# Where the weight buffers and the activation buffers of a two-layer decoder trunk begin in SBUF

## The chip, the cores and the metric

The kernel runs on one core of a Trainium2 chip. The metric is device time in microseconds (us) from the start to the end of one execution. Three executions of the kernel before took 626.92, 623.93 and 623.89 us; the median is 623.93 us.

## The reference

The reference is a decoder trunk of two layers on 256 tokens of 1024 features, all in float32. Every sub-layer is x + gate * f(rmsnorm(x) * (1 + scale) + shift), where shift, scale and gate are columns of silu(c) @ w_ada + b_ada.

```
for i in range(2):
    sh_m, sc_m, g_m, sh_f, sc_f, g_f = split(silu(c) @ w_ada[i] + b_ada[i], 6)
    h = rmsnorm(x) * (1 + sc_m) + sh_m
    y = attention(h)          # layer 0: 8 heads, causal, QK norm
        or short_conv(h)      # layer 1: (B * conv3(C * u)) @ w_out
    x = x + g_m * y
    h = rmsnorm(x) * (1 + sc_f) + sh_f
    x = x + g_f * ((silu(h @ w_gate) * (h @ w_up)) @ w_down)   # d_ff = 2816
```

## The kernel before

**The products.** Each float32 operand of a large product is held as two float32r parts: a high part and the rest. A product then takes three matmuls (`mm3`, lines 287 to 289): high by high, high weight by low moving, low weight by high moving. Each loads its own 128 x 128 stationary operand and streams 256 columns of 1024 bytes per partition past it. There are 4704 such matmuls. 

**The weights.** They come from HBM in chunks of 256 columns, in the order of their use. A chunk lands in a `wf` buffer (five of them); ScalarE writes its high part into a `wh` tile and VectorE the rest into a `wl` tile (`prep`, `split_w`, lines 88 to 99). There are three `wh` and three `wl` buffers, taken in turn, and each part of a chunk is 8192 bytes per partition. A chunk is asked for two chunks ahead of its use (`produce`, `get`).

**The activations.** They lie feature-major in pairs of tiles, a high and a low part. `new_pair("h", ...)` holds the modulated input of a sub-layer: q, k, v, gate, up and the convolution's input products read it (names `m0`, `f0`, `m1`, `f1`). `new_pair("a", ...)` holds the 22 x 256 values between up and down projection, which the down projection reads (`a0`, `a1`, output `op_d`). `wide_pair` holds tag `z`: the attention's output and the convolution's output, read by the two output projections (`ov`, `zv`, outputs `op_o`, `op_co`). The first gate and up chunks of a sub-layer work on a raw pair, which lies at the end of an `a` pair or in a `z` pair and has 258 columns, so that its eight blocks begin 1032 bytes apart (outputs `raw_f`, `raw_m`).

**Where the tiles lie.** The tiles of a pool are laid one behind the other, in the order in which their tags are first asked for, each starting at a multiple of 32 bytes. Behind the five `wf` buffers come the three `wh`, the three `wl`, and then the activations `al`, `zh`, `xT`, `hh`, `hl`, `zl`, `ah`. All of them are a multiple of 128 bytes long but `zh` and `zl`, which have 8256 bytes (64.5 times 128).

**What sets the order.** TensorE works through its instructions in the program's order; where each chunk's split and load stand on ScalarE, VectorE and SyncE's DMA queue follows from `get` and `produce`. A `wh` or `wl` buffer is written again once the products of the chunk three turns earlier have read it.

Of the kernel before, what the change touches and what calls it, by code (L numbers as in the profile page):

```python
# [15 lines left out]
P = 128  # L16
S = 256
# [14 lines left out]
def trunk_kernel(ctx: ExitStack, tc: tile.TileContext, x, c, w_ada, b_ada, norm_mix, norm_ffn, w_qkv, w_o,  # L32
# [20 lines left out]

# [1 line left out]
    crow = const.tile([KD, P], F32, name="crow")  # L55
# [24 lines left out]

# [1 line left out]
    def load(src, nk, ncol, name):  # L82
# [3 lines left out]
        return flat  # L86

    def prep(src, nk, name):
        wf = load(src, nk, CW, "wf_" + name)
        wh = wpool.tile([P, 8, CW], F32R, tag="wh", name="wh_" + name, bufs=3)  # L90
        wl = wpool.tile([P, 8, CW], F32R, tag="wl", name="wl_" + name, bufs=3)
        split_w(wf, wh, wl, nk)
        return wh, wl
# [6 lines left out]

# [1 line left out]
    mod = const.tile([P, DEPTH * 48], F32, name="mod")  # L102
# [3 lines left out]
    def ada_piece(l, part, i):  # L106
        w = load(w_ada[l, i * 256:(i + 1) * 256, part * D:(part + 1) * D], 2, D, f"wa_{l}_{part}_{i}")
        if i == 0:
            acc_of[l, part] = tmp.tile([P, D], F32, tag="acc", name=f"acc_{l}_{part}", bufs=1)
        acc = acc_of[l, part]  # L110
        for kk in range(2):
            k = 2 * i + kk
            if k == 0:
                nc.vector.tensor_scalar(acc, w[:, kk], sc[:, k:k + 1], None, op0=ALU.mult)
            else:
                nc.vector.scalar_tensor_tensor(acc, w[:, kk], sc[:, k:k + 1], acc, op0=ALU.mult, op1=ALU.add)  # L116
        if i < 3:
            return
        if l == 0 and part != G_F:
            late.append((gets[0], lambda: ada_end(l, part, acc)))  # L120
            return
        # the sum over the partitions, of three bfloat16 parts that add up to the float32 values: less for PE
        parts = [tmp.tile([P, D], BF16, tag=f"part{n}", name=f"part{n}_{l}_{part}", bufs=1) for n in range(3)]
        for n, p in enumerate(parts):
            if n < 2:
                nc.scalar.activation(p, acc, AF.Copy)
                nc.vector.tensor_sub(acc if n == 0 else parts[2], acc, p)
        late.append((gets[0], lambda: ada_end_parts(l, part, parts)))

    def ada_end(l, part, acc):  # L130
        # the sum over the partitions, on four groups of 32 columns of the array at once: less for DVE and ScalarE
        ps = ps_misc(f"mod_ps_{l}_{part}")[:, :2 * P]
        for g in range(4):
            nc.tensor.matmul(ps[32 * g:32 * g + 32], one.to_broadcast([P, 32]), acc[:, g * 2 * P:(g + 1) * 2 * P],
                             start=True, stop=True, skip_group_check=True, tile_position=(0, 32 * g))
        y = tmp.tile([P, 2, P], F32, tag="t", name=f"mod_y_{l}_{part}", bufs=3)
        nc.scalar.activation(y, ps.rearrange("p (i c) -> p i c", c=P), AF.Copy)

        def end():
            ps = ps_misc(f"mod_c_{l}_{part}")  # L140
            for i in range(2):
                nc.tensor.transpose(ps[:, i * P:(i + 1) * P], y[:, i], ident)
            mod_from(ps[:, :2 * P].rearrange("p (i g r) -> p g i r", i=2, r=32)[:, :, :, 0], l, part)

        return end
# [41 lines left out]

    rows = act.tile([P, 3 * P], F32, tag="al", name="rows")
    brow, vrow, grow = (rows[:n, i * P:(i + 1) * P] for i, n in enumerate((DEPTH * 48, 42, 16)))
    x_flat = act.tile([P, KD * (S + 2)], F32, tag="zh", name="x_tok")  # L190
    x_tok = x_flat[:, :2 * D].rearrange("p (t d) -> p t d", d=D)
# [16 lines left out]

# [1 line left out]
    chunks = []  # L210
# [72 lines left out]

# [1 line left out]
    def mm3(ps, lhs, rhs, first, last):  # L285
# [25 lines left out]
    def new_pair(tag, name, nk):  # L311
        return (act.tile([P, nk, S], F32R, tag=tag + "h", name=name + "h"),
                act.tile([P, nk, S], F32R, tag=tag + "l", name=name + "l"))

    # A raw pair holds x * (1 + scale) * gain, not yet over its norm, and the shift as one more token (twice, for an
    # even number of them). Products of it need no norm; rstd and the product of the shift come to them afterwards:
    # (x A rstd + sh) W = (x A) W rstd + sh W.
    RAW = KD * (S + 2)

    def wide_pair(name):  # L320
        flat = [act.tile([P, RAW], F32R, tag="z" + p, name=name + p) for p in "hl"]
        return (tuple(f[:, :KD * S].rearrange("p (k s) -> p k s", s=S) for f in flat),
                tuple(f.rearrange("p (k s) -> p k s", s=S + 2) for f in flat))
# [4 lines left out]

# [1 line left out]
    xT = act.tile([P, KD, S], F32, name="xT")  # L330
# [20 lines left out]
    class Norm:  # L351
        """Sums of squares over the features, gathered as the residual's tiles come."""

# [83 lines left out]
    def raw_gemm(keys, norm, name):  # L437
        """Two chunks' products of the raw pair; returns (product * rstd, the shift's product) of each, and
        the modulated pair. The norm's own products come in between."""
        raw = norm.raw  # L440
# [43 lines left out]

# [1 line left out]
    def mod_sums(w, name):  # L486
        # Four groups of 32 columns of the array hold four rows of c at once: partial sums in four groups of partitions.
        n = w.shape[1]
        ps = ps_misc("mod_ps_" + name)
        psv = ps[:, :n * P].rearrange("p (n c) -> p n c", c=P)  # L490
        for k in range(KD):
            g = 32 * (k % 4)
            nc.tensor.matmul(psv[g:g + 32], sc[:, k:k + 1].to_broadcast([P, 32]), w[:, :, k], start=k < 4, stop=k >= 4,
                             skip_group_check=True, tile_position=(0, g))
        y = tmp.tile([P, 2, P], F32, tag="t", name="mod_y_" + name, bufs=3)[:, :n]
        nc.vector.tensor_copy(y, psv)
        return y

    def group_sums(ps, y, name):
        # the four groups' partial sums added up, as columns  # L500
        n = y.shape[1]
# [37 lines left out]
    def w_operands(k, wf):  # L539
        ops = (wpool.tile([P, 8, CW], F32R, tag="wh", name=f"wh_qk_{k}", bufs=3),  # L540
               wpool.tile([P, 8, CW], F32R, tag="wl", name=f"wl_qk_{k}", bufs=3))
        w_part(wf, ops, 0, 2)
        return ops
# [6 lines left out]
    def first_products(k, ops, js):  # L550
        wh, wl = ops
        for j in js:
            for t in range(2):
                ts = slice(t * P, (t + 1) * P)
                # q feature-major, k token-major
                if j < 4:
# [9 lines left out]
    def keep_warm(n):  # L566
        # The array's clock falls while it idles: products that nothing reads keep it up until the first operands are there.
        ps = ps_misc("warm")
# [4 lines left out]
    with tc.manual_schedule(engines={mybir.EngineType.PE, mybir.EngineType.DVE, mybir.EngineType.Activation}):  # L573
# [4 lines left out]
        nc.vector.tensor_copy(mask_r, causal)  # L578
        # brings the table of square roots in before the first one is needed
        std = const.tile([P, 2], F32, name="std0")  # L580
        nc.scalar.activation(std[:, 0:1], eps, AF.Sqrt)
        keep_warm(14)
        w_ada0, wf = first
        sq = act.tile([P, RAW], F32, tag="zl", name="sq0")
        ssq = const.tile([P, 2], F32, name="ssq0")
# [50 lines left out]

# [1 line left out]
    qT = act.tile([P, 2, H, S], F32, tag="ah", name="qkT")  # L638
    vp = act.tile([P, 2 * D + H * 3 * P], F32, tag="al", name="vp")
    v_sb = vp[:, :2 * D].rearrange("p (t d) -> p t d", d=D)  # L640
# [23 lines left out]
    def q_sums(ps, a):  # L664
        # Four heads at once, on 32 columns of the array each: their sums end in four groups of partitions.
        for g in range(4):
# [73 lines left out]

    # The attention's own steps run between the products of the k and v chunks, each late enough to find its operands.
    ahead = get(("k", 2))
# [37 lines left out]

# [1 line left out]
    ups = [act.tile([P, 2, S + 2], F32, tag=f"up{i}", name=f"up{i}") for i in range(2)]  # L782
# [37 lines left out]

# [1 line left out]
    of = out[0].rearrange("(t p) d -> p t d", p=P)  # L822
# [43 lines left out]
```

## Time and profile before

| | |
|---|---|
| median of three runs | 623.93 us |
| span of the profiled execution | 622.1 us (1.8 us below the median) |
| TensorE matmul busy | 609.7 us, 98% |
| TensorE weight load busy | 595.8 us, 96% |
| VectorE busy | 473.6 us, 76% |
| ScalarE busy | 323.1 us, 52% |
| DMA, mean | 251 GB/s, 156.07 MB |

A page of the profile has one line for each engine, the span in 40 slices, the chain of work that ended last, and the costliest groups of instructions. Durations of matmuls overlap, since the array is pipelined: how fast TensorE advances is the time from the start of one matmul to the start of the next, not its duration. In a stretch without gaps it is the length of the stretch over the number of matmuls in it.

### The profile page before, as it was taken

To read this page: it belongs to the slowest core of one execution; us is meant where nothing else is said; L and a number is where in the kernel's file an instruction comes from. 1 tells how busy PE (TensorE), PEld (TensorE's weight loads), DVE (VectorE), ACT (ScalarE), POOL (GpSimd) and SP (SyncE) were. 2 spreads that over 40 slices of the span, in tenths; PEclk is the share of its full clock that TensorE was granted. 3 is DMA by queue.
4 is the path that set the end of the run, shared out by engine and by line. 5 is a ranking of instruction groups with operands and counts; after the bars stand their busy time and mean duration, and the time that the engine had idled before them with its cause. 6 is when DMAs were issued, how large, how long until landed. Compare 5 with 4: busy or idle time off the path is not lost.

```text
span 622.1 us, 12512 instructions
## 1 busy us (share of the span) xinstructions
PE 609.7 (98%) x5291; PEld 595.8 (96%) x5291; DVE 473.6 (76%) x668; ACT 323.1 (52%) x518; POOL 19.2 (3%) x26
## 2 busy tenths in 40 slices
PE   7999999999999999999999999999999999999997
PEld 5789999999999999999999999998999999999997
DVE  5567999989989899979888989658976467644440
ACT  5335977466655455535355745545744435533330
POOL 0000000020000000000110000012000000000000
PEclk9999999999999999999999999999999999999999
DMA  9999999966699999798998497646388677655200
GB/s 271 329 331 354 385 370 335 303 219 223 210 323 322 347 333 335 257 318 303 319 302 278 133 304 241 210 138 205 108 299 271 201 225 235 204 188 178 94 18 17
DMA packets 127455, 156.07 MB, mean 251 GB/s; under 512 B 2822, under 2 KB 114856, under 8 KB 127400
## 3 DMA queue, kind: packets, MB, share of 16 engines
q1 hardware_dynamic: 127400, 155.28, 75.6%
q8 instruction: 41, 0.67, 0.5%
q14 instruction: 14, 0.11, 0.1%
HBM read 154.22 MB, written 1.05 MB: 250 GB/s over the span
## 4 chain that ended last, share of the span: by engine, by line
PE 88%; DMA 3%; DVE 3%; issue 3%; ACT 1%; SPq 0%; POOLq 0%; POOL 0%; ACTq 0%
PE pu L289 7%; PE pu L288 7%; PE op_d L287 7%; PE pu L287 7%; PE op_d L289 7%; PE op_d L288 7%; PE pg L289 6%; PE pg L288 6%; PE pg L287 6%; DMA wa<-in_w_ada_dram 2%; DMA wf_qk<-in_w_qkv_dram 1%; PE pv L287 1%; PE pb L288 1%; PE pv L289 1%; PE pb L287 1%
## 5 line engine op out<-in xcount | busy, mean ns | idle before, releaser
L116 DVE SCALAR_TENSOR_TENSOR acc<-wa,sc,acc 128x1024 f32<-128x1024 f32 x70 | 89.8, 1283 | 8.8 <-DMA wa<-in_w_ada_dram 7.5
L98 ACT ACTIVATE wh_d<-wf_d 128x1024 fp32r<-128x1024 f32 (+1 forms) x48 | 45.5, 981 | 69.7 <-issue 47.2
L99 DVE TENSOR_TENSOR wl_d<-wf_d,wh_d 128x1024 fp32r<-128x1024 f32 (+1 forms) x48 | 53.6, 1144 | 30.7 <-ACT wh_d L98 30.5
L98 ACT ACTIVATE wh_u<-wf_u 128x1024 fp32r<-128x1024 f32 x44 | 44.3, 1051 | 45.3 <-issue 34.5
L98 ACT ACTIVATE wh_g<-wf_g 128x1024 fp32r<-128x1024 f32 x44 | 45.5, 1050 | 40.7 <-issue 40.7
L99 DVE TENSOR_TENSOR wl_u<-wf_u,wh_u 128x1024 fp32r<-128x1024 f32 x44 | 52.7, 1233 | 14.0 <-ACT wh_u L98 14.0
L99 DVE TENSOR_TENSOR wl_g<-wf_g,wh_g 128x1024 fp32r<-128x1024 f32 x44 | 54.5, 1245 | 2.1 <-ACT wh_g L98 2.0
L287 PE MATMUL op_d<-a1h,wh_d 128*128 128x256 f32 x176 | 50.3, 286 | 0.0
L287 PE MATMUL op_d<-a0h,wh_d 128*128 128x256 f32 x176 | 50.2, 285 | 0.0
L289 PE MATMUL op_d<-a1h,wl_d 128*128 128x256 f32 x176 | 50.0, 284 | 0.0
L289 PE MATMUL op_d<-a0h,wl_d 128*128 128x256 f32 x176 | 50.0, 284 | 0.0
L288 PE MATMUL op_d<-a1l,wh_d 128*128 128x256 f32 x176 | 49.6, 282 | 0.0
L288 PE MATMUL op_d<-a0l,wh_d 128*128 128x256 f32 x176 | 49.5, 281 | 0.0
L289 PE MATMUL pg<-f1h,wl_g 128*128 128x256 f32 x160 | 44.8, 280 | 0.0
L289 PE MATMUL pu<-f1h,wl_u 128*128 128x256 f32 x160 | 44.8, 280 | 0.0
L287 PE MATMUL pg<-f1h,wh_g 128*128 128x256 f32 x160 | 44.6, 279 | 0.0
L288 PE MATMUL pg<-f1l,wh_g 128*128 128x256 f32 x160 | 44.6, 279 | 0.0
L287 PE MATMUL pu<-f1h,wh_u 128*128 128x256 f32 x160 | 44.6, 279 | 0.0
L288 PE MATMUL pu<-f1l,wh_u 128*128 128x256 f32 x160 | 44.6, 279 | 0.0
L287 PE MATMUL pg<-f0h,wh_g 128*128 128x256 f32 x160 | 44.5, 278 | 0.0
L289 PE MATMUL pg<-f0h,wl_g 128*128 128x256 f32 x160 | 44.4, 278 | 0.0
L289 PE MATMUL pu<-f0h,wl_u 128*128 128x256 f32 x160 | 44.4, 278 | 0.0
(315 smaller groups left out, 2103.6 us busy)
## 6 DMA issues: line engine op xcount, KB each, us to landing
wa<-in_w_ada_dram SPq DMA_DIRECT2D x40, 1024.0 KB, 6.1
wf_g<-in_w_gate_up_dram SPq DMA_DIRECT2D x22, 1024.0 KB, 6.6
wf_u<-in_w_gate_up_dram SPq DMA_DIRECT2D x22, 1024.0 KB, 7.5
wf_d<-in_w_down_dram SPq DMA_DIRECT2D x16, 1024.0 KB, 6.3
wa<-in_w_ada_dram SPq DMA_DIRECT2D x16, 512.0 KB, 7.1
wf_d<-in_w_down_dram SPq DMA_DIRECT2D x8, 768.0 KB, 5.7
wf_qk<-in_w_qkv_dram SPq DMA_DIRECT2D x8, 512.0 KB, 8.1
wf_v<-in_w_qkv_dram SPq DMA_DIRECT2D x4, 1024.0 KB, 7.5
```

Source lines behind the costliest of these rows:

```text
L98: nc.scalar.activation(wh[:, a:b], wf[:, a:b], AF.Copy)
L99: nc.vector.tensor_sub(wl[:, a:b], wf[:, a:b], wh[:, a:b].bitcast(F32))
L116: nc.vector.scalar_tensor_tensor(acc, w[:, kk], sc[:, k:k + 1], acc, op0=ALU.mult, op1=ALU.add)
L287: nc.tensor.matmul(ps, ah, bh, start=first, stop=False, skip_group_check=True)
L288: nc.tensor.matmul(ps, ah, bl, start=False, stop=False, skip_group_check=True)
L289: nc.tensor.matmul(ps, al, bh, start=False, stop=last, skip_group_check=True)
```

## The change

All `wh`, `wl` and activation tiles are taken a little larger, and the data begins some floats into the tile. The three `wh` and the three `wl` buffers become six tags with one buffer each, taken in the same turn. Offsets in the code count floats of 4 bytes. Comments and empty lines that the diff also drops are left out here.

```diff
+    turn_of = {"h": 0, "l": 0}
+
+    def w_tile(part, name):
+        i = turn_of[part] % 3
+        turn_of[part] += 1
+        a = (0, 4, 0)[i]
+        flat = wpool.tile([P, 8 * CW + (8 if part == "l" and i == 2 else (0, 32, 32)[i])], F32R, tag=f"w{part}{i}", name=f"w{part}_{name}", bufs=1)
+        return flat[:, a:a + 8 * CW].rearrange("p (k c) -> p k c", c=CW)
+
     def prep(src, nk, name):
         wf = load(src, nk, CW, "wf_" + name)
-        wh = wpool.tile([P, 8, CW], F32R, tag="wh", name="wh_" + name, bufs=3)
-        wl = wpool.tile([P, 8, CW], F32R, tag="wl", name="wl_" + name, bufs=3)
+        wh, wl = w_tile("h", name), w_tile("l", name)
...
+    OFF = {"ah": 12, "al": 12 - 8, "z": 24, "h": 0}
+
+    def room(tag, n, name, dtype=F32):
+        size = {"ah": KF * S + 32, "al": KF * S + 32 - 8}.get(tag) or {"z": 2112, "h": KD * S + 0}[tag[0]]
+        o = OFF.get(tag, OFF.get(tag[0]))
+        return act.tile([P, size], dtype, tag=tag, name=name)[:, o:o + n]
+
-    rows = act.tile([P, 3 * P], F32, tag="al", name="rows")
+    rows = room("al", 3 * P, "rows")
...
-    x_flat = act.tile([P, KD * (S + 2)], F32, tag="zh", name="x_tok")
+    x_flat = room("zh", KD * (S + 2), "x_tok")
...
     def new_pair(tag, name, nk):
-        return (act.tile([P, nk, S], F32R, tag=tag + "h", name=name + "h"),
-                act.tile([P, nk, S], F32R, tag=tag + "l", name=name + "l"))
...
+        return tuple(room(tag + p, nk * S, name + p, F32R).rearrange("p (k s) -> p k s", s=S) for p in "hl")
...
     def wide_pair(name):
-        flat = [act.tile([P, RAW], F32R, tag="z" + p, name=name + p) for p in "hl"]
+        flat = [room("z" + p, RAW, name + p, F32R) for p in "hl"]
...
     def w_operands(k, wf):
-        ops = (wpool.tile([P, 8, CW], F32R, tag="wh", name=f"wh_qk_{k}", bufs=3),
-               wpool.tile([P, 8, CW], F32R, tag="wl", name=f"wl_qk_{k}", bufs=3))
+        ops = w_tile("h", f"qk_{k}"), w_tile("l", f"qk_{k}")
...
-        sq = act.tile([P, RAW], F32, tag="zl", name="sq0")
+        sq = room("zl", RAW, "sq0")
...
-    qT = act.tile([P, 2, H, S], F32, tag="ah", name="qkT")
-    vp = act.tile([P, 2 * D + H * 3 * P], F32, tag="al", name="vp")
+    qT = room("ah", 2 * H * S, "qkT").rearrange("p (a h s) -> p a h s", a=2, h=H)
+    vp = room("al", 2 * D + H * 3 * P, "vp")
```

## Rows read from the trace of the kernel before

**Rows 1.** The page: busy time, clock and DMA by slices, the chain that ended last.
```profile
PE 609.7 (98%) x5291; PEld 595.8 (96%) x5291; DVE 473.6 (76%) x668; ACT 323.1 (52%) x518; POOL 19.2 (3%) x26
...
PEclk9999999999999999999999999999999999999999
...
PE 88%; DMA 3%; DVE 3%; issue 3%; ACT 1%; SPq 0%; POOLq 0%; POOL 0%; ACTq 0%
```

**Rows 2.** Busy time by stretches: stretch, length, engines (instructions), clock, DMA share, GB/s.
```profile
155.00:197.00 42.00, 42.00 (x358) 42.00 (x358) 38.93 (x46) 25.45 (x31) 0.00 (x0) 1.00 0.79 272
202.00:232.00 30.00, 30.00 (x267) 30.00 (x266) 27.14 (x26) 14.69 (x18) 0.00 (x0) 1.00 1.01 339
268.00:298.00 30.00, 30.00 (x252) 30.00 (x252) 27.19 (x29) 13.24 (x17) 0.89 (x1) 1.00 0.90 306
345.00:400.00 55.00, 55.00 (x469) 55.00 (x469) 47.28 (x64) 30.56 (x40) 0.00 (x0) 1.00 0.71 230
403.00:412.00 9.00, 9.00 (x77) 9.00 (x76) 1.87 (x4) 0.31 (x1) 0.00 (x0) 1.00 0.55 179
440.00:500.00 60.00, 60.00 (x512) 60.00 (x511) 42.46 (x50) 30.75 (x38) 0.00 (x0) 1.00 0.70 228
69.80:73.80 4.00, 4.00 (x38) 4.00 (x37) 3.93 (x5) 3.04 (x15) 0.00 (x0) 1.00 1.07 354
148.50:154.10 5.60, 5.60 (x49) 5.60 (x48) 5.35 (x14) 3.64 (x8) 0.00 (x0) 1.00 0.95 344
```

**Rows 3.** Timeline of TensorE around 199.5 us: start, duration, instruction.
```profile
199.12 0.28 PE L288 MATMUL pu<-f0l,wh_u 128*128 128x256 f32 x1
199.24 0.28 PE L289 MATMUL pu<-f0h,wl_u 128*128 128x256 f32 x1
199.36 0.75 PE L151 MATMUL mod_ps<-one_b,part 128*128 128x1 bf16 x24
199.97 0.36 PE L287 MATMUL pg<-f0h,wh_g 128*128 128x256 f32 x1
200.17 0.28 PE L288 MATMUL pg<-f0l,wh_g 128*128 128x256 f32 x1
200.28 0.28 PE L289 MATMUL pg<-f0h,wl_g 128*128 128x256 f32 x1
200.40 0.28 PE L287 MATMUL pg<-f0h,wh_g 128*128 128x256 f32 x1
```

**Rows 4.** Tiles: instructions, count, duration in ns (least, median, greatest), where.
```profile
L287 PE MATMUL pg<-f0h,wh_g x160: 276/276/363, 154.1 to 260.3; 128*128 128x256 f32 x160
L288 PEld LDWEIGHTS op_d<-a0l,wh_d x176: 187/189/193, 266.7 to 330.4; 128*128 128x128 f32 x176
L287 PE MATMUL op_d<-a0h,wh_d x176: 284/284/364, 266.7 to 330.4; 128*128 128x256 f32 x176
L289 PE MATMUL raw_f<-a0h,wl_u x16: 276/284/293, 142.5 to 154.0; 128*128 128x258 f32 x16
```

**Rows 5.** Groups of matmuls with their counts: count, busy us, mean ns.
```profile
L287 PE MATMUL op_d<-a1h,wh_d 128*128 128x256 f32 x176 | 50.3, 286 | 0.0
...
L289 PE MATMUL pg<-f1h,wl_g 128*128 128x256 f32 x160 | 44.8, 280 | 0.0
...
L287 PE MATMUL op_co<-zvh,wh_co 128*128 128x256 f32 x64 | 18.3, 286 | 0.0
...
L288 PE MATMUL pb<-m1l,wh_cb 128*128 128x256 f32 x64 | 17.9, 280 | 0.0
...
L288 PE MATMUL pc<-m1l,wh_cg 128*128 128x256 f32 x48 | 13.4, 280 | 0.0
```

**Rows 6.** Stretch of the q and k products (columns as in rows 2).
```profile
25.00:61.00 36.00, 35.33 (x324) 30.98 (x322) 25.17 (x64) 16.27 (x29) 0.00 (x0) 1.00 1.12 338
```

**Rows 7.** Waits: who waited for whom, us in total, times, longest.
```profile
ACT wh_g L98 <- issue: 40.7, 14, 3.2
...
ACT wh_d L98 <- PE op_d L288: 22.6, 7, 4.1
```

## The prediction

> **What bounds the kernel now.** I read the page first: TensorE's matmuls are busy 98% of the span at the full granted clock in every slice, and TensorE holds 88% of the chain that ended last, against 3% each for DMA and VectorE [rows 1]. Matmul durations overlap, so I then read the windows, where a stretch without gaps gives the time from one matmul to the next. A window also counts the matmuls that straddle its edges; one lasts 0.28 us, which at these rates is 2.4 more than start in it. The gate and up products of layer 0 thus take 42.00/(358 - 2.4) = 118.1 ns each up to 197 us and 30.00/(267 - 2.4) = 113.4 ns from 202 us on; those of layer 1 60.00/(512 - 2.4) = 117.7 ns; the convolution's 55.00/(469 - 2.4) = 117.9 ns; the down projection 30.00/(252 - 2.4) = 120.2 ns; the convolution's output projection 9.00/(77 - 2.4) = 120.6 ns [rows 2]. All these matmuls have the same shape, kind and clock, and TensorE and its weight load have no gap in any of these stretches. So the bound has three levels, 113.4, about 118 and 120.2 ns, and the change can only act on them.
>
> What separates the levels? Not the weight buffer: each stretch runs through all three. Not the other engines: VectorE is busy 38.93 of 42 us in the 118.1 ns stretch and 27.14 of 30 in the 113.4 ns one, with more DMA beside the latter (share 1.01 against 0.79) [rows 2]. Two things are left. One is history: the step from 118 to 113 ns comes right behind 24 short matmuls at 199.36 us, with the same buffers before and after [rows 3]. The other is where the two operands lie. In multiples of 128 bytes, take the beginning of the weight buffers as 0. Adding up the tile sizes, `al`, `zh` and `ah` are at 0 before; `zh`'s half multiple puts `hh`, `hl` and `zl` at 64; all steps from block to block inside these tiles are multiples of 128. Every product of an `h` pair therefore has its two operands 64 bytes apart, and runs at 113.4 or about 118; every product of an `a` pair has them 0 apart, and runs at 120.2; the output projections have 0 for the high part and 64 for the low one, and run at 120.6 where I could measure them. In the down projection the weight load itself is sometimes held up: 187 to 193 ns, median 189, and its matmuls have a median of 284 ns where the gate's have 276 [rows 4].
>
> **The change, part by part.** *The layout.* Each part of it again in multiples of 128, from the sizes in the diff: `wh` and `wl` of turn 0 at 0; turn 1 at 16, in tiles of 8320 = 65 times 128 bytes; turn 2 at 0, where `wl`'s 8224 bytes push what follows by 32. `al` begins at 32 + 16 = 48, and its 22624 bytes bring the next tile back to 0. `zh` and `zl` lie at 96 in tiles of 8448 = 66 times 128; `hh` and `hl` at 0; `ah` at 48. So the distance of the two operands becomes
>
> - `h` pairs: 64 before; after it 0 in turns 0 and 2, and 16 in turn 1;
> - `a` pairs: 0 before; after it 48, 32 and 48;
> - `z` pairs: 0 and 64 before; after it 96, 80 and 96 for both parts.
>
> The change takes from the `h` products the distance that goes with the low levels, and gives them in two turns of three exactly that of the down projection.
>
> *The `h` products.* I count them from the groups: 12 groups of 160 for gate and up, three groups of 48 each for two of the convolution's inputs and three of 64 for the third [rows 5], that is 1920 + 480. Gate and up of layer 0: 8 chunks of 48 at 118.1 go to 120.2, 384 x 2.1 ns = 0.8 us; 12 chunks at 113.4, 576 x 6.8 = 3.9 us. Layer 1: 960 x 2.5 = 2.4 us. Convolution: 480 x 2.3 = 1.1 us. The remaining 576 are q, k and v. Half of them lie where the stream of weights has a DMA share of 1.12 and the weight load is busy 30.98 of 36 us [rows 6]; there I take 0, since TensorE waits anyway. For the other half I take 3.7 ns, from the mean over gate and up, (384 x 118.1 + 576 x 113.4 + 960 x 117.7)/1920 = 116.5, to 120.2: 1.1 us. Sum 9.3 us, all on the path, because nothing lies over TensorE. This charges turn 1, whose distance of 16 bytes no steady stretch shows, like the others: that is my value, nearest to the row at 0 by distance. Its ends: 113.4 for a third of 2976 products, 992 x 6.8 = 6.7 us less; and 9 ns more than a 120.2 ns matmul, as the longest raw matmul is over the median of its row (293 against 284 [rows 4]), 8.9 us more.
>
> *The `a` products*: 6 groups of 176 [rows 5], 1056. No steady stretch has 48 or 32 bytes. Their ends are the least and the present level, 113.4 and 120.2, so -7.2 to 0 us. If what counts is in which half of the 128 bytes each operand begins, they move from the same half to opposite halves, as the `h` pairs have it today; I take the `h` pairs' mean of 116.5: 1056 x 3.7 = -3.9 us. *The `z` products*: 2 x 192, from 0 and 64 to one distance near 96: 0, with ends of -2.8 us (113.4) and +0.1. *The raw blocks*: 288 products, whose 1032-byte steps make them pass through distances from 64 up in steps of 8. The last half of one, distances 96 to 120, takes 5.60/(49 - 2.4) = 120.2 ns [rows 2]. They pass through as many others afterwards: 0, with -2.0 us (113.4) as the good end and 288 x 9 ns = 2.6 us as the bad one.
>
> *Everything else*: the same instructions in the same order. Six tags of one buffer are taken in the turn in which the two tags of three were; a split waits for the same chunk's products as before. Were a buffer to come later, ScalarE's slack covers it: it sat idle 40.7 us before `wh_g` splits that waited for nothing, and its 22.6 us of waiting for the down projection's buffers left no gap in TensorE [rows 2, 7]. ScalarE and VectorE work at new offsets; below that is covered by 3 us of idle VectorE in the tightest 42 [rows 2], and if the cover were gone each percent on VectorE there would be 0.4 us.
>
> A rule that speaks against all this: in the rows, equal matmuls run at 113.4 and 120.2 ns, and the weight load stretches with them [rows 2, 4]. The Trainium skill, "TensorE: Matmul & The Clock Gate", section "Step-by-step: what each phase is for", says that TensorE has two independent read ports into SBUF, so that loading the next weights takes no bandwidth from the running matmul; by it the sum would be 0 and the time 623.9 us. The two levels in these rows speak for the ports meeting somewhere behind.
>
> **Sum.** 9.3 - 3.9 + 0 + 0 = +5.4 us, on a span of 622.1: 627.5. The median is 1.8 us over the profiled span, which I carry: 629.3 us. The ends of this case: 9.3 - 6.7 - 7.2 - 2.8 - 2.0 = -9.4, if all that is unknown falls to the lowest level at once, and 9.3 + 8.9 + 0 + 0.1 + 2.6 = +20.9, if all that is unknown falls on the bad side. As these are several independent ends I take 624 to 638 for this case.
>
> **Rivals.** *All distances but 0 and 64 are good (faster).* A distance that isn't a multiple of 64 lets the two streams slip past each other, turn 1's 16 bytes sets the right phase, and the turns at 0 keep it, as the 113.4 ns level was kept through the whole stretch to 232 us after one push [rows 2, 3]. For it: a level once reached persists through all buffers. Against it: the raw blocks pass through many distances and run at 120.2. It decides the sign once the `a` pairs and turn 1 both reach 113.4: 9.3 - 7.2 - 6.7 = -4.6. It would give back (118.1 - 113.4) x 384 = 1.8, 4.3 x 960 = 4.1, 4.5 x 480 = 2.2, 6.8 x 1056 = 7.2, 7.2 x 384 = 2.8, 6.8 x 288 = 2.0 and about 0.9 for v: 21.0 us, 602.9 us. *The weight buffers don't matter, only the activations' place (faster).* `h` stays at its levels, `a` and `z` fall to 113.4: -7.2 - 2.8 = -10.0, 613.9 us. For it: `a` is the highest level now. Against it: in k the activation is the loaded operand and the weight the streamed one, the places change roles, and the products still run at 4.00/(38 - 2.4) = 112 ns from 69.8 us [rows 2]. *Offsets do nothing.* The levels are history alone, set anew at each interruption like that at 199.36 us: 623.9 us. Against it: the down projection's window is at the high level throughout, and none of the five windows on `h` is [rows 2].
>
> **How the numbers follow.** Likeliest case 0.66, all at 113.4 0.12, activations alone 0.10, no effect 0.12. About 0.5%, or 3.1 us, is what a measurement of this kernel can tell from no change: within 620.8 to 627.0 lie the no-effect case and 0.04 of the likeliest one, 0.16; faster 0.22; slower 0.62. The range from 613 to 638 leaves out the first rival and the likeliest case's upper tail.
>
> **What would show it.** Right: gate and up in both layers at 120.2 ns from matmul to matmul in all three turns, also behind the 24 short matmuls; matmul medians of 282 to 285 ns there and weight loads up to 193; the down projection at 118 or 113.4 with loads of 188. Wrong: any long gate or up stretch at 113.4, or a down projection still at 120.2. If turn 1 differs from turns 0 and 2, every third chunk shows another level. A gap in TensorE beyond those of today would mean that the sum left out a wait.

## The result, and the profile after

The changed kernel took 628.55 us, the median of six runs (627.75 to 629.85), the kernel before 624.64 us on the same chip (six runs, 623.76 to 626.99). The ratio is 1.006, with a 95% interval of 1.0035 to 1.0084: 3.9 us slower, and the interval does not reach down to 1. The forecast was 629.3 us, slower by 5.4. The profiled execution took 629.01 us with a span of 627.2 us, 5.1 us longer than the span before. Three of the six executions of the changed kernel had a mean granted clock of 1.0 and took 627.75 to 628.08 us; the other three, the profiled one among them, had 0.996 or 0.997 and took 629.01 to 629.85 us.

The lines of the page of the changed kernel that answer to [rows 1]:

```profile
PE 615.3 (98%) x5291; PEld 601.9 (96%) x5291; DVE 474.1 (76%) x668; ACT 322.1 (51%) x518; POOL 19.3 (3%) x26
...
PEclk9999999999999999999999999998999999999999
...
PE 88%; DMA 3%; issue 3%; DVE 3%; ACT 1%; SPq 0%; POOLq 0%; POOL 0%; ACTq 0%
```

The same instructions in the same order, and TensorE still carries 88% of the chain. ScalarE and VectorE have not moved (322.1 and 474.1 us against 323.1 and 473.6): the longer time is in TensorE's products. TensorE's idle time did not grow (span less busy time: 11.9 us against 12.4). One slice shows a clock below full; it comes back below.

The stretches of the changed kernel that answer to [rows 2], columns as there:

```profile
156.00:198.00 42.00, 42.00 (x355) 42.00 (x354) 38.65 (x45) 25.15 (x31) 0.00 (x0) 1.00 0.79 270
203.00:233.00 30.00, 30.00 (x254) 30.00 (x254) 26.98 (x27) 14.82 (x18) 0.00 (x0) 1.00 0.98 331
272.50:300.00 27.50, 27.50 (x238) 27.50 (x237) 25.09 (x27) 13.26 (x17) 0.90 (x1) 1.00 0.87 287
349.00:404.00 55.00, 55.00 (x464) 55.00 (x463) 46.62 (x63) 29.47 (x39) 0.00 (x0) 1.00 0.72 230
445.00:505.00 60.00, 60.00 (x507) 60.00 (x505) 41.86 (x49) 30.68 (x38) 0.00 (x0) 1.00 0.70 228
```

Read as before, length over count less 2.4 (a count is off by up to one, 0.4% of a stretch of 30 us): gate and up of layer 0 119.1 and 119.2 ns on the two sides of the 24 short matmuls (before 118.1 and 113.4), the down projection 116.7 (120.2), the convolution 119.2 (117.9), gate and up of layer 1 118.9 (117.7). The 113.4 ns stretch is gone, and the down projection is now the fastest of the long stages.

The tiles that answer to [rows 4], and with them one of layer 1's down projection, also of the kernel before, that the working below needs. Each row has count, least, median and greatest duration in ns, and the first and the last start in us. First the changed kernel:

```profile
L303 PE MATMUL pg<-f0h,wh_g x160: 277/282/363, 154.9 to 264.6; 128*128 128x256 f32 x160
...
L304 PEld LDWEIGHTS op_d<-a0l,wh_d x176: 187/188/192, 271.4 to 333.4; 128*128 128x128 f32 x176
...
L303 PE MATMUL op_d<-a0h,wh_d x176: 277/278/366, 271.3 to 333.4; 128*128 128x256 f32 x176
...
L303 PE MATMUL op_d<-a1h,wh_d x176: 277/279/363, 558.9 to 622.3; 128*128 128x256 f32 x176
```

Then the kernel before:

```profile
L287 PE MATMUL op_d<-a1h,wh_d x176: 274/284/364, 552.6 to 617.1; 128*128 128x256 f32 x176
```

The medians have changed places: the gate's went from 276 to 282 ns, the down projection's from 284 to 278, and the weight load of the latter from 189 to 188.

The turns show in the starts of the chunks. TensorE's timeline of the changed kernel, the first matmul of five gate and up chunks, 48 matmuls from each to the next (start in us, duration in us):

```profile
166.40 0.28 PE L303 MATMUL pg<-f0h,wh_g 128*128 128x256 f32 x1
...
172.09 0.28 PE L303 MATMUL pu<-f0h,wh_u 128*128 128x256 f32 x1
...
177.81 0.28 PE L303 MATMUL pg<-f0h,wh_g 128*128 128x256 f32 x1
...
183.56 0.28 PE L303 MATMUL pu<-f0h,wh_u 128*128 128x256 f32 x1
...
189.25 0.28 PE L303 MATMUL pg<-f0h,wh_g 128*128 128x256 f32 x1
```

The lengths are 5.69, 5.72, 5.75 and 5.69 us: 118.5 ns a matmul in turn 1 (16 bytes apart), 119.2 in the turn behind it, 119.8 in the next, and again. Only the second chunk in a row at distance 0 comes near the 120.2 ns that the prediction charged to all.

The slice with the lower clock is layer 1's raw block. TensorE's timeline and two windows of the changed kernel, the first matmul of the norm's sums, the first of the 24 raw matmuls behind them, and the first behind those:

```profile
432.53 0.38 PE L402 MATMUL ms_n<-inv_d,ss_n 128*128 128x1 f32 x2 [1.61 <-POOL ss_n L382]
...
433.45 0.36 PE L303 MATMUL raw_f<-a1h,wh_g 128*128 128x258 f32 x1
...
438.05 0.37 PE L303 MATMUL raw_f<-a1h,wh_g 128*128 128x258 f32 x1
...
433.00:436.00 3.00, 3.00 (x22) 3.00 (x22) 1.37 (x3) 0.26 (x1) 0.00 (x0) 0.77 0.63 204
436.00:439.00 3.00, 3.00 (x20) 3.00 (x19) 0.25 (x1) 0.38 (x1) 0.00 (x0) 0.67 0.94 321
```

The same in the kernel before:

```profile
428.99 0.38 PE L387 MATMUL ms_n<-inv_d,ss_n 128*128 128x1 f32 x2 [1.04 <-POOL ss_n L367]
...
429.90 0.37 PE L287 MATMUL raw_f<-a1h,wh_g 128*128 128x258 f32 x1
...
433.00 0.36 PE L287 MATMUL raw_f<-a1h,wh_g 128*128 128x258 f32 x1
```

TensorE had stood still for 1.61 us before the norm's sums (the number in brackets), and behind them the granted clock fell for a while to the lower of its two levels, 1.2 GHz. The 24 raw matmuls took 438.05 - 433.45 = 4.60 us, where the kernel before, at full clock in every slice [rows 1], took 433.00 - 429.90 = 3.10: 1.5 us of the profile's 5.1.

### The profile page after: what moved, and what is told of

It is laid out like the page before. It is cut to its first block, busy times and chain, and to the rows that moved or that the text cites. A ratio compares the mean times of both kernels' runs of the same rounds, so it can differ in the third digit from the quotient of the medians.

```text
span 627.2 us, 12516 instructions
## 1 busy us (share of the span) xinstructions
PE 615.3 (98%) x5291; PEld 601.9 (96%) x5291; DVE 474.1 (76%) x668; ACT 322.1 (51%) x518; POOL 19.3 (3%) x26
## 4 chain that ended last, share of the span: by engine, by line
PE 88%; DMA 3%; issue 3%; DVE 3%; ACT 1%; SPq 0%; POOLq 0%; POOL 0%; ACTq 0%
PE pu L304 7%; PE pu L303 7%; PE pu L305 7%; PE op_d L303 7%; PE op_d L305 7%; PE op_d L304 7%; PE pg L303 6%; PE pg L304 6%; PE pg L305 6%; DMA wa<-in_w_ada_dram 2%; DMA wf_qk<-in_w_qkv_dram 1%; PE pv L303 1%; PE pb L304 1%; PE pb L303 1%; PE pb L305 1%
## 5 line engine op out<-in xcount | busy, mean ns | idle before, releaser
L304 PE MATMUL pg<-f0l,wh_g 128*128 128x256 f32 x160 | 45.2, 282 | 0.0
L304 PE MATMUL pu<-f0l,wh_u 128*128 128x256 f32 x160 | 45.2, 282 | 0.0
L303 PE MATMUL pu<-f0h,wh_u 128*128 128x256 f32 x160 | 45.1, 282 | 0.0
```

The lines of the kernel that those rows point to most:

```text
L303: nc.tensor.matmul(ps, ah, bh, start=first, stop=False, skip_group_check=True)
L304: nc.tensor.matmul(ps, ah, bl, start=False, stop=False, skip_group_check=True)
```

## The experiments

My theory was that the interval between matmuls depends on how far apart the two operands begin within 128 bytes; the rivals were history alone, the offset of turn 1 by itself, and later the absolute place. Each time below is a median, with the ratio to the kernel before, run on the same chip. All kernels have the instructions of the changed kernel; only addresses differ.

**h alone back to 64.** Against the changed kernel; shorter `z` tiles (65.5 times 128 bytes) put `hh` and `hl` back to 64:

```diff
-    OFF = {"ah": 12, "al": 12 - 8, "z": 24, "h": 0}
+    OFF = {"ah": 12, "al": 12 - 8, "zh": 24, "zl": 24 - 16, "h": 0}
...
-        size = {"ah": KF * S + 32, "al": KF * S + 32 - 8}.get(tag) or {"z": 2112, "h": KD * S + 0}[tag[0]]
+        size = {"ah": KF * S + 32, "al": KF * S + 32 - 8}.get(tag) or {"z": 2112 - 16, "h": KD * S + 0}[tag[0]]
```

> The changed kernel with the h pairs alone put back to 64 bytes from the weights of turns 0 and 2 (48 from turn 1). Theory (what counts is whether the two operands of a product begin in the same or in opposite halves of 128 bytes): gate and up leave 120.0 ns and come back to 113.4 to 118 ns from matmul to matmul, the down projection keeps the 117 ns that it has in the changed kernel; against the kernel before that is 1056 x (120.2 - 117) = 3.4 us less, about 621 us, some 7 us under the changed kernel. Rival (turn 1's offset in the weights itself costs, through ScalarE and VectorE or through the array): every third chunk stays at 118 ns or more and the rest comes back, about 624. Rival (history alone): gate and up stay at 119 to 120 ns, about 628.

620.27 us, 0.9918 [0.9897, 0.9938]: 8.3 us under the changed kernel. Its chunks, columns as in the timeline above:

```profile
165.41 0.28 PE L303 MATMUL pg<-f0h,wh_g 128*128 128x256 f32 x1
...
171.06 0.28 PE L303 MATMUL pu<-f0h,wh_u 128*128 128x256 f32 x1
...
176.54 0.28 PE L303 MATMUL pg<-f0h,wh_g 128*128 128x256 f32 x1
...
181.98 0.28 PE L303 MATMUL pu<-f0h,wh_u 128*128 128x256 f32 x1
```

5.65, 5.48 and 5.44 us: turn 1, 48 apart, runs at 117.7 ns, the turns at 64 apart at 114.2 and 113.3. So the loss of the change is the `h` pairs' distance, as theory said. But the good turns are better than before (118.1 in this stretch, [rows 2]), at the same distance. And the down projection, whose distances are those of the changed kernel, did not keep the 117 ns expected; its window in layer 0 gives 118.3:

```profile
268.00:296.00 28.00, 28.00 (x239) 28.00 (x238) 25.25 (x27) 13.39 (x17) 0.91 (x1) 1.00 0.90 300
```

**Turn 1 at 0.** Against the changed kernel:

```diff
-        a = (0, 4, 0)[i]
+        a = (0, 0, 0)[i]
```

> The changed kernel with turn 1's weights at offset 0 like those of turns 0 and 2: the h pairs have distance 0 in every turn. Theory (halves, and the 16 bytes of turn 1 help a little): all gate and up chunks at 120.0 ns; the mean over three turns is 119.2 in the changed kernel, so 2976 x 0.8 ns = 2.4 us slower than it, about 631 us. The a pairs go from 48/32/48 to 48 throughout: within 0.5 us. Rival (turn 1 is what disturbs: each change of phase throws the other turns onto the high level): without it gate and up come down to 118 or 113.4, 4 to 19 us faster than the changed kernel. Rival (history alone): some long stretch of gate and up off 120.0.

628.77 us, 1.0058 [1.0039, 1.0077]: as the changed kernel. The theory had asked for 2 us more. Gate and up of layer 0 and 1:

```profile
156.00:198.00 42.00, 42.00 (x354) 42.00 (x353) 38.67 (x46) 25.51 (x32) 0.00 (x0) 1.00 0.79 267
...
445.00:505.00 60.00, 60.00 (x506) 60.00 (x505) 41.66 (x50) 30.07 (x37) 0.00 (x0) 1.00 0.71 228
```

119.5 and 119.1 ns. Turn 1's 16 bytes do neither good nor harm, and distance 0 alone does not hold a stretch at 120.2. This kernel also has the pause in layer 1's raw block, and kept the full clock behind it:

```profile
431.00:434.00 3.00, 1.51 (x13) 1.30 (x13) 3.00 (x6) 2.47 (x5) 1.45 (x1) 1.00 0.61 203
434.00:437.00 3.00, 3.00 (x27) 3.00 (x27) 1.16 (x2) 0.26 (x1) 0.00 (x0) 1.00 0.63 196
```

So a pause like that one (1.49 of 3 us idle here) can pass without the fall, and three of the changed kernel's own six executions kept the full clock too: the low clock in its profile is not the layout's.

**a alone at 64.** Against the changed kernel; the weight tiles have no room behind their data, so that this is the layout before but for `al` and `ah`:

```diff
-        a = (0, 4, 0)[i]
+        a = (0, 0, 0)[i]
...
-    OFF = {"ah": 12, "al": 12 - 8, "z": 24, "h": 0}
+    OFF = {"ah": 16, "al": 16, "z": 0, "h": 0}
...
+        size = {"ah": KF * S + 32, "al": KF * S + 32}.get(tag) or {"z": KD * (S + 2), "h": KD * S + 0}[tag[0]]
```

> The kernel before with the a pairs alone moved, from 0 to 64 bytes from the weights; h, z and the weights stay. Theory (halves): the down projection leaves 120.2 ns for one of the two levels that the h pairs have at 64 apart, 117.8 or 113.4: 1056 x 2.4 = 2.5 us or 1056 x 6.8 = 7.2 us faster than the kernel before, 617 to 622 us; gate and up as before. Rival (history alone): down projection still at 120.2, time as before. Rival (only distances that aren't multiples of 64 help): still at 120, time as before.

619.42 us, 0.9906 [0.9888, 0.9925]: 6.0 us faster. Two parts of layer 0's down projection, and the convolution:

```profile
270.00:298.00 28.00, 28.00 (x240) 28.00 (x239) 25.31 (x26) 13.04 (x17) 0.91 (x1) 1.00 0.94 318
303.00:330.00 27.00, 27.00 (x241) 27.00 (x240) 24.07 (x24) 13.04 (x16) 1.89 (x2) 1.00 0.93 306
345.00:393.00 48.00, 48.00 (x426) 48.00 (x426) 42.27 (x57) 27.76 (x36) 0.00 (x0) 1.00 0.76 247
```

The down projection runs at 117.8 ns up to the short matmuls near 298 us and at 113.2 behind them; the convolution, whose layout is that of before, at 113.3 instead of 117.9. From the first start of a stage to the first start of the next, the trace's down projections are 2.33 and 1.03 us shorter than those of the kernel before, and the convolution 2.12: 5.5 of the 6.0 us. So a pair at 64 has two levels, a stretch keeps one until something interrupts it, and a change in one stage moves another stage's level.

**All at 64.** Against the kernel above, with 64 bytes more behind the last `wl`:

```diff
-    OFF = {"ah": 16, "al": 16, "z": 0, "h": 0}
+    OFF = {"ah": 0, "al": 0, "z": 0, "h": 0}
...
+        size = {"ah": KF * S, "al": KF * S}.get(tag) or {"z": KD * (S + 2) + 16, "h": KD * S + 0}[tag[0]]
```

> The kernel before with every activation pair (h, a, z) 64 bytes from the weights, all turns alike. Theory (halves): down projection as in the run that moves a alone, and the output projections (384 matmuls, now 120.6) at 117.8 or 113.4 as well: another 0.9 to 2.8 us. Together 3.4 to 10 us faster than the kernel before, 615 to 621 us; which of the two levels a stretch takes is open. Rival (history alone): as before. Rival (the whole pattern of before is a balance, and moving zh also moves the attention's operands): slower in the attention's stretch by more than 1 us.

625.68 us, 1.0012 [0.9997, 1.0026]: no gain, where 615 to 621 us were expected. Behind the 24 short matmuls in layer 0, and in layer 0's down projection:

```profile
202.00:232.00 30.00, 30.00 (x258) 30.00 (x257) 26.73 (x26) 14.46 (x18) 0.00 (x0) 1.00 0.99 333
270.50:299.50 29.00, 29.00 (x249) 29.00 (x248) 26.36 (x28) 13.37 (x17) 0.90 (x1) 1.00 0.89 296
```

117.4 and 117.6 ns: the distance is right and every stretch sits on the upper of the two levels. Distance says which levels there are. Which of them a stretch has is not drawn anew in each execution: the 17 executions of the kernel before that were timed beside this one took 623.77 to 624.11 us at a granted clock of 0.998 or more, 625.40 to 625.60 at 0.996 and 626.76 to 626.96 at 0.994, and its 113.4 ns stretch at 118 (576 x 4.6 ns) would be 2.6 us more at equal clock. So the level goes with the kernel and not with the single execution; what in the kernel decides, no run isolates.

**The absolute place.** Three layouts moved on by 32 bytes as a whole: that of before, that of all_at_64, and one with every pair at distance 0. In each the first `wh` tile's data begins 8 floats later, in a tile 8 floats longer, so that all tiles behind it move too. The third has no unmoved twin:

```diff
+        a = 8 if part == "h" and i == 0 else 0
```

> The kernel before with all weight and activation tiles moved on by 32 bytes together: every distance as before, but by the program's map of addresses the weights now begin at a multiple of 128 bytes instead of at 96 behind one, and the activations at 0 or 64 instead of 96 or 32. Theory A (only the distance of the two operands counts): all stretches as before, 113.4 to 120.2 ns, time as before. Theory B (the place itself counts too): the levels 113.33 and 120.0 ns are 17 and 18 times 6.67 ns, and a moving operand of 1024 bytes is 16 pieces of 64 bytes; begun at 32 behind a multiple of 64 it touches 17 such pieces, begun at one only 16. Then every level falls by one piece of 6.67 ns at most, to 106.7 to 113.5 ns: 4704 x 3 to 6.7 ns = 14 to 31 us faster, about 595 to 611 us.

> Every activation pair 64 bytes from the weights, as in the run all_at_64, and all moved on by 32 bytes: weights at 0, activations at 64 of 128. Theory A (distance alone): 117.8 ns throughout as in all_at_64, or 113.3 where an interruption throws it there; 610 to 626 us. Theory B (place too): lower than both levels everywhere, 106.7 to 113.3 ns; against all_at_64 4704 x 4.5 to 11 ns less, 574 to 604 us.

> Every activation pair at distance 0 from the weights, and all at multiples of 128 bytes. Theory A (distance alone): 120.0 ns throughout as the changed kernel's h products in turns 0 and 2; 2976 x 3.3 ns = 10 us slower than the kernel before, about 635 us. Theory B (place too): 113.3 ns or less, 4704 x 5 ns faster than the kernel before, about 600 us; if with B the distance counts no more, the same time as all_at_64_32_on.

626.90 us, 1.0037 [1.0024, 1.005]; 623.50 us, 0.9987 [0.9974, 1.0]; 630.64 us, 1.0099 [1.0076, 1.0123]. Theory B is out: no stretch came below the levels known, where it asked for 106.7 to 113.5 ns. Theory A's 635 us for the third was 4 too high. Stretches of before_32_on, of all_at_64_32_on and of all_at_0_32_on (for the last gate and up, then down projection):

```profile
202.00:232.00 30.00, 30.00 (x258) 30.00 (x256) 26.70 (x25) 14.70 (x17) 0.00 (x0) 1.00 0.99 331
```
```profile
202.00:232.00 30.00, 30.00 (x257) 30.00 (x256) 27.11 (x26) 14.70 (x18) 0.00 (x0) 1.00 0.98 332
236.50:264.50 28.00, 28.00 (x249) 28.00 (x249) 26.01 (x26) 14.81 (x18) 0.00 (x0) 1.00 0.87 286
```
```profile
156.50:198.50 42.00, 42.00 (x356) 42.00 (x356) 38.84 (x46) 24.79 (x30) 0.00 (x0) 1.00 0.82 276
...
272.50:301.50 29.00, 29.00 (x244) 29.00 (x243) 25.83 (x26) 12.98 (x16) 0.90 (x1) 1.00 0.87 288
```

before_32_on has every distance of before, and where that ran at 113.4 ns [rows 2] it runs at 117.4: 576 x 4 ns = 2.3 of the 2.5 us that it lost. Its convolution's output projection went the other way, 22.7 us from its first start to the next stage's where the kernel before takes 23.1, at the same distances. all_at_64_32_on changes from 117.8 to 113.5 at a second group of short matmuls near 235 us. At distance 0 no stretch is at 113: 118.8 for gate and up (119.1 to 119.5 in turn1_at_0, also at 0) and 120.0 for the down projection.

**A push from the activations.** Theory now: the step from 48 to 64 leads to the good level, as behind every turn 1 of h_at_64_again. Against all_at_64, block 0 of an `h` pair and blocks 0 and 1 of an `a` pair lie at 28 floats plus their number times 256, the others at 32:

```diff
+            o = 28 if a < self.n else 32
+            v = self.flat[:, o + a * S:o + b * S]
```

> The kernel all_at_64, but block 0 of each h pair and blocks 0 and 1 of each a pair lie 16 bytes earlier, 48 from the weights, so that every chunk of gate, up and convolution and every output of the down projection begins with a few products at 48 and goes on at 64. Theory (at 64 apart a stretch keeps one of two phases, 113.3 or 117.8 ns, and the step from 48 to 64 always leads to the good one, as after every turn 1 of h_at_64_again): seven eighths of gate, up and convolution at 113.3, one eighth at 117.8, mean 113.9; the down projection likewise from 117.8 to 113.7: 2400 x 3.9 + 1056 x 4.1 = 13.7 us less than all_at_64 (625.7), about 612 us. Rival (the good phase in h_at_64_again came from the weights' place in turn 1 or from its buffers, not from the step of distance): 117.8 throughout, about 625 us. Rival (the level is set only by interruptions of the stream): some stretches at 113.3, others at 117.8, 615 to 625 us, and chunks of one stretch all alike.

625.53 us, 1.0007 [0.9993, 1.0022]. Gate and up of layer 0 and 1:

```profile
156.00:198.00 42.00, 42.00 (x359) 42.00 (x358) 38.93 (x47) 24.60 (x30) 0.00 (x0) 1.00 0.82 278
...
442.00:502.00 60.00, 60.00 (x512) 60.00 (x511) 42.36 (x50) 30.84 (x38) 0.00 (x0) 1.00 0.71 228
```

117.8 and 117.7 ns throughout, as the first rival said. What this rules out is a step of this length: the push lasts 6 of a chunk's 48 matmuls, turn 1 of h_at_64_again lasted all 48.

**A push from the weights.** Against all_at_64, only turn 1: the first half of a chunk's blocks begins 4 floats into the tile, the second half 32:

```diff
+            o = 4 if a < self.n else 32
+            v = self.flat[:, o + a * CW:o + b * CW]
```

> The kernel all_at_64, but in turn 1 the first half of the weights' blocks lies 16 bytes later, 48 from the activations, the second half at 64 as in the other turns. Theory (the step from 48 to 64 leads to the good phase and the phase then stays): one sixth of the products at 117.8, five sixths at 113.3, mean 114.1; against all_at_64 some 3400 x 3.7 = 12.7 us less, about 613 us; only the chunks between an interruption and the next turn 1 may be at 117.8. Rival (a half chunk is too short, or the step within a chunk does nothing): 117.8 throughout, 625 us. Rival (interruptions alone set the level): 615 to 625 us, with whole stretches alike.

615.57 us, 0.9844 [0.9823, 0.9866]. The first matmuls of the chunks, and behind the first of them the 25th matmul of the pushed chunk:

```profile
165.52 0.28 PE L313 MATMUL pg<-f0h,wh_g 128*128 128x256 f32 x1
...
168.35 0.28 PE L313 MATMUL pg<-f0h,wh_g 128*128 128x256 f32 x1
...
171.20 0.28 PE L313 MATMUL pu<-f0h,wh_u 128*128 128x256 f32 x1
...
176.64 0.28 PE L313 MATMUL pg<-f0h,wh_g 128*128 128x256 f32 x1
...
182.08 0.28 PE L313 MATMUL pu<-f0h,wh_u 128*128 128x256 f32 x1
```

5.68, 5.44 and 5.44 us: 118.3 ns in the pushed chunk, 113.3 in the two behind it. So 16 bytes on the side of the weights do what they did not on the side of the activations; but this push is also four times as long, 24 matmuls, and no run has equal lengths on both sides. The pushed chunk stays slow to its end: its first half, 48 apart, takes 2.83 us and its second, back at 64, 2.85 (118.8 ns). The step from 48 to 64 inside the chunk thus did not lead to 113.3 here; that came with the next chunk. Half a chunk costs what a whole one does (117.7 in h_at_64_again).

**All at 72.** Against all_at_64, `OFF` is 2 floats for all, with tiles 128 bytes longer for `h` and `a`:

```diff
+    OFF = {"a": 2, "z": 2, "h": 2}
```

> Every activation pair 72 bytes from the weights in all turns, 8 more than in all_at_64. Theory (64 apart has two phases, and a distance a little off it no longer has the bad one): 113.3 ns throughout, 4.5 x 4400 = 20 us less than all_at_64, about 605 us. Theory (every distance that is no multiple of 64 mixes good and bad meetings, as 48 in the changed kernel and in turn 1 of h_at_64_again): 116 to 118.5 ns, 620 to 628 us. Rival (distance does not matter beyond the half): the two levels of 64, by stretches.

630.62 us, 1.0082 [1.0066, 1.0097]: slower than either theory said. Gate and up, then down projection, of layer 0:

```profile
159.00:201.00 42.00, 42.00 (x355) 42.00 (x354) 37.12 (x45) 24.31 (x30) 0.00 (x0) 1.00 0.80 266
...
275.00:303.00 28.00, 28.00 (x236) 28.00 (x235) 24.79 (x25) 12.95 (x16) 0.91 (x1) 1.00 0.85 280
```

119.1 and 119.9 ns: eight bytes off 64 both lower levels are gone. This also rules out the rule of the halves: 72 puts the two operands into opposite halves of 128 bytes just as 64 does.

**Few pushes.** Against all_at_64, weight tiles 128 bytes longer and the whole chunk 4 floats later in 11 chunks:

```diff
+    PUSH = {"g_0_1", "g_0_5", "g_0_8", "d_0_0_0", "d_0_2_0", "cb_0", "g_1_1",
+            "d_1_0_0", "d_1_1_0", "d_1_2_0", "d_1_3_0"}
...
+        a = 4 if name in PUSH else 0
```

> The kernel all_at_64, with the weights 16 bytes later in 11 chunks alone: the first h chunk behind each raw block, the chunk behind each group of short matmuls, and the first chunk of those outputs of the down projection that an interruption precedes. Theory (a stretch at 64 apart keeps its phase until it is interrupted, and one chunk with the weights 16 bytes on leads to the good one): 113.3 ns in all gate, up, convolution and down projection chunks but these 11. Against 64_with_push_in_turn_1, where some 24 chunks run at 116 to 118 ns, that is 13 to 16 chunks x 48 x 4.9 ns = 3 to 4 us less, about 612 us. Rival (the good phase decays by itself and has to be set anew every third chunk): gate and up of layer 1 come back to 117.8 somewhere behind their one push, 615 to 622 us. Rival (the push works only in turn 1's buffers): pushes in other turns leave 117.8, 618 to 625 us.

614.75 us, 0.9841 [0.9819, 0.9863]. Layer 1's gate and up behind their one push, and layer 0's down projection behind its first:

```profile
442.50:542.50 100.00, 100.00 (x885) 100.00 (x884) 69.48 (x69) 49.92 (x60) 0.00 (x0) 1.00 0.75 243
...
273.00:296.00 23.00, 23.00 (x196) 23.00 (x195) 22.30 (x23) 12.02 (x16) 0.90 (x1) 1.00 0.90 304
```

113.3 ns for 100 us, so the level does not decay. Pushes work in any turn: of those in gate, up and convolution one fell in turn 0, one in turn 2, three in turn 1. But a whole pushed chunk led five of the down projection's six stretches to a third level, 118.8 ns in the row above, and the gain over 64_with_push_in_turn_1 was 0.8 us instead of 3 to 4.

**Few pushes, half a chunk in the down projection.** Against the kernel above:

```diff
+        if a and name[0] == "d":
+            return Halves(flat, 4)
```

where the first four blocks begin at 4 floats and the rest at 32, as in 64_with_push_in_turn_1.

> The kernel 64_with_few_pushes, but in the pushed chunks of the down projection only the first half of the blocks lies 16 bytes later. In 64_with_few_pushes a whole pushed chunk led five of the six stretches of the down projection to 118.9 ns, in 64_with_push_in_turn_1 half a chunk led all eight to 113.3. Theory (where the push ends sets the phase, and a half push ends at the good place for a pairs): the chunks behind the pushed ones at 113.3 ns, (5 x 44 + 8 x 42) x 5.6 ns = 3.1 us less than 64_with_few_pushes, about 611.7 us. Rival (in layer 1 what stands ahead of the push decides too, since the transposes of the output come in there): layer 0 at 113.3, layer 1 still at 118.9 or 117.8, about 613.5 us. Rival (chance at each interruption): a mix within a layer, 612 to 616 us.

611.74 us, 0.9797 [0.978, 0.9815]: the fastest kernel here, 12.3 us under the kernel before on its chip and 16.8 under the changed one, which was timed on another. The down projections of layer 0 and 1 behind a push:

```profile
273.00:296.50 23.50, 23.50 (x210) 23.50 (x208) 22.41 (x23) 12.29 (x16) 0.90 (x1) 1.00 0.91 302
...
565.20:574.70 9.50, 9.50 (x86) 9.41 (x84) 5.60 (x6) 4.00 (x5) 0.00 (x0) 1.00 0.38 118
```

113.2 and 113.6 ns (the second window is short, so a count off by one makes 1.2%), as the theory said.

## Why the prediction was right, and where its terms were off

**The bound and the mechanism: right.** TensorE's matmul interval is what changed, and the `h` pairs' distance is what changed it: put back alone it gave 8.3 us, more than it had cost, because the stretches also came to another level than before. The forecast of slower by 5.4 us met 3.9 by the medians. Two errors that offset each other in part helped it: the loss on the `h` products was put 2.7 us too high, the gain on the `a` products 1.2.

The two traces, each stage from its first start to the first start of the next (us):

| stage | before | after | longer | forecast |
|---|---|---|---|---|
| all up to the output projection (q, k, v) | 112.37 | 113.14 | 0.8 | 1.1 |
| gate and up, layer 0 | 112.53 | 116.38 | 3.8 | 4.7 |
| convolution | 57.15 | 57.85 | 0.7 | 1.1 |
| gate and up, layer 1 | 113.68 | 114.98 | 1.3 | 2.4 |
| two output projections | 50.72 | 50.36 | -0.4 | 0 |
| raw blocks | 41.34 | 43.09 | 1.7 | 0 |

**The `h` term, +9.3 us: too large, 6.6 measured.** The first of its four rows is the weakest: before_32_on, with the distances of the kernel before, reaches the output projection 0.5 us earlier than that kernel. The step that was mis-sized is the charge of 120.2 ns to all turns: I took the level of the down projection for the level of distance 0. The chunks of one round average (118.5 + 119.2 + 119.8)/3 = 119.2 ns, and 1.0 ns on the 2400 gate, up and convolution products is 2.4 of the 2.7 us. Turn 1 is not the reason, since without its 16 bytes the time is the same; distance 0 has more than one level too.

**The `a` term, -3.9 us: the sign right, -2.7 measured, the reason wrong.** From first to last start the down projection went from 63.7 us [rows 4] to 62.1 in layer 0 and from 64.5 to 63.4 in layer 1, 3.0 and 2.1 ns a product instead of 3.7. The prediction took the `h` pairs' mean on the condition that the half of the 128 bytes counts in which each operand begins. (By its own offsets, weights at 0 and `a` pairs at 48, both begin in the same half; only with the weights at 96 behind a multiple of 128, as the expectation for before_32_on has it, are the halves opposite.) It does not count so: at 72, in opposite halves too, the down projection ran at 119.9 ns and gate and up at 119.1 (all_at_72). That 48 and 32 came near 116.5 was luck; in h_at_64_again the same distances gave 118.3.

**`z` and raw: near 0.** The two output projections are 0.4 us shorter together. Of the raw blocks' 1.7 us 1.5 are the low clock of this one execution. **Everything else:** right. ScalarE and VectorE are as busy as before, and TensorE's idle time did not grow. The terms measured make 6.6 - 2.7 - 0.4 + 0.2 = 3.7 us, near the 3.9 of the medians and the 5.1 - 1.5 = 3.6 of the spans.

**What was to show it.** Gate and up did not come to 120.2 ns in all turns: every third chunk showed another level, and only one turn came near it. They did come to 282 ns medians and lost their 113.4 ns behind the short matmuls, and the down projection came to 188 ns loads.

**The rivals.** That the activations' place alone matters fell with gate and up, which lost and did not stay. That all distances but 0 and 64 are good fell with turn 1 (118.5 ns) and all_at_72. That offsets do nothing fell with h_at_64_again; with it falls the rule of the Trainium skill, "TensorE: Matmul & The Clock Gate", section "Step-by-step: what each phase is for", as the prediction read it for this case: if the place of the operands could not matter between the two read ports, these kernels would have taken one time, and they took 611.7 to 630.6 us. But that rival held half of the truth. In the `a` term and for q, k and v I had taken 113.4 and 118 ns as one mean for 64 apart; they are two levels at one distance, and something else than the distance chooses: before_32_on lost 2.5 us with no distance changed. Here luck helped the sum: about 3.3 of the 6.6 us (576 x 5.8 ns) come from the one stretch that happened to stand at 113.4 ns and could only lose. Against before_32_on, where it stands at 117.4, the ratios (1.006 and 1.0037) leave the change a cost of only some 1.4 us.

**Open.** No run shows what in the chip makes the levels, nor what chooses among those of one distance: the stretch's past, as its changes at interruptions suggest, or the place of the tiles beyond the distance within 128 bytes, which also differs between before, before_32_on and all_at_64. Nor is it shown why a push from the weights leads to the good level and a push from the activations does not: they differ in side, in length (24 or 48 matmuls against 6) and in how often they come, and 16 bytes the other way were not tried.

## What to carry to other kernels

Where TensorE is the bound and loads new weights for each matmul, look at the matmul interval by stretches, and at the offsets of both operands within 128 bytes: 64 apart was the only distance here at which 113.3 ns was reached for long, against 117 to 120 ns at 0, 16, 48 and 72. Then look whether equal products run at two levels in one trace; if they do, a layout that is right on paper can sit at the wrong one, and a few chunks at another offset behind each interruption can set it. Treat one good stretch as luck until another kernel with the same distances has it too: more executions of the same kernel only repeat its level.

## What the runs showed of the hardware that I had not expected

- One layout has several lasting levels: 113.3 and 117.8 ns at 64 apart, with 118.8 behind a whole pushed chunk of the down projection. A level outlasted 100 us and all three weight buffers, changed at groups of short bfloat16 matmuls or behind chunks with the weights 16 bytes on, and was the same in the 17 executions of the kernel before, as far as their times tell.
- Moving everything by 32 bytes brought no new level (before_32_on, all_at_64_32_on), though it changed which level some stretches took.
- 113.2 to 113.3 ns was the least that any long stretch reached, in the twelve runs as in the kernel before.
- After 1.6 us without a matmul the granted clock fell to 1.2 GHz for part of the next 6 us in the profile of the changed kernel, which cost 1.5 us; behind a pause at the same place and of about the same length turn1_at_0 kept full clock.
